# Three pairs of PSUM banks in turn for a windowed attention, and one bank each for its projections and its values

## The chip, the cores and the metric

The kernel runs on one core of one Trainium2 chip. The metric is the device time of one execution in microseconds, here the median of three runs of the kernel before: 1449.96 us (1449.54 to 1451.34).

## What is computed

A trunk of two layers over 1024 latent tokens (a grid of 16 rows and 64 columns) and 256 context tokens, width 1024, 16 heads of 64, all in float32. The change lies in the first layer, a windowed attention with grouped keys, a sink logit for each head and a gate. Cut to what matters:

```python
q, k, v, g = _split_a(u @ w_in)                    # latents; uc likewise, without rotation
q = apply_axial_rope(q, rope); k = apply_axial_rope(k, rope)
for each block of 128 queries and each head:
    s = [q @ k(own block and its two neighbours), masked; q @ k(context); sink]
    p = softmax(s * HEAD_DIM ** -0.5)
    o = p_lat @ v + p_ctx @ v_ctx
y = (o * silu(g)) @ w_out
h = layer_norm(ALPHA * h + gate * y)
```

Context queries look at the context alone. The second layer is a neighbourhood attention of the same build.

## The kernel before, in words

Numbers keep their precision by being split into a high and a low part: a projection makes three matmuls for each 128 rows of its weights (high by high, high by low, low by high, lines 208 to 210).

**Phases of the first layer.** First the modulated tokens `uA`, the keys and part of the values are made; then the attention runs over 8 pairs of heads `p`, each with 10 blocks of 128 tokens (8 of latents, 2 of context) and 2 heads, that is 20 units a pair and 160 in all. Beside the attention of pair `p` run, as filling, the projections of its gate and of the next pair's queries (`gprojA(p)`, `qprojA(p + 1)`). A projection goes over three chunks of tokens (`CHUNKS`: 512, 512 and the 256 of the context), 24 matmuls each, into a PSUM tile `pj`. The chunks of one run are named `pj<j>_<c>`: `pj32` is a query projection, `pj34` the gate projection after it.

**A unit of the attention.** `qkA` makes the scores `S_A` on TensorE (lines 704, 705). `sm_first` scales, masks and reduces them on VectorE (line 317, a custom instruction with the read of its accumulator into `m_A`), then ScalarE takes the exponential (line 324); `sm_second` takes the reciprocal `rs_A` on VectorE (line 328) and GpSimd multiplies (line 329). `sm_transpose` transposes the probabilities on TensorE into `T_A` (line 336), ScalarE copies the high part out (`pth_A`, line 340) and VectorE subtracts for the low part (`ptl_A`, line 342). `pvA_fn` multiplies with the values into a `pvA` tile (line 733), which two blocks share; two ScalarE copies and two VectorE additions (`otmp`, lines 742, 743) empty it. The scores run three units ahead of the transposes (`AHEAD_A = 3`).

**What empties a projection's tile.** For the queries `rope_evac`: VectorE shuffles `pj` into `rb` (line 469), multiplies `pj` by the cosine into `ra` (line 470), GpSimd multiplies `rb` by the sine (line 471), VectorE adds (line 472), and `q_store` makes for each of the two heads a ScalarE cast (line 659) and a VectorE subtraction (line 660) into `qA`. The chunk of the context isn't rotated: `q_store` reads it straight from PSUM. For the gate `g_evac`: ScalarE takes a tanh of `pj` into a tile with the tag `ra` (line 277), VectorE combines it with `pj` into `gA` (line 278). In the first layer the tags `ra` and `rb` have one buffer each.

**PSUM.** [...] The pool `ps` has two tiles of two banks (tag `big`: scores, transposes, sums of the output projection) and four of one bank (tag `one`: projections, values and the rest). A tile gets the buffer that comes free.

**Other work on the same engines.** VectorE and GpSimd work on 48 dot products for the modulation of later steps (`dots`, lines 617, 618, tile `gj`), 7 of them in most pairs.

**What sets the order.** Each engine runs its instructions in the order in which they stand in its program. A scheduler makes that order when the kernel is built, by priorities (order of emission, `merge` mixes attention and filling; `lift(n)` raises what is inside it by n places) and by when it takes buffers to be free. On the chip an instruction waits for semaphores, and all that stands behind it on its engine waits too.

Of the kernel before, what the change touches and what calls it, by code (L numbers as in the profile page):

```python
# [11 lines left out]
F32 = mybir.dt.float32  # L12
# [4 lines left out]
PSUM = bass.MemoryType.PSUM  # L17
DRAM = bass.MemoryType.DRAM

P = 128  # L20
D = 1024
S = 1024
# [8 lines left out]
CHUNKS = ((0, 512), (512, 512), (1024, 256))  # L31
# [2 lines left out]

AHEAD_A, LIFT_A = 3, 80
AHEAD_B, LIFT_B = 3, 40
BARE_B = 108

GATED_LAST = 1 << 20
# [43 lines left out]
def build(tc, i, out):  # L83
    nc = tc.nc
# [7 lines left out]
        return p, st  # L92

    dr = es.enter_context(tc.tile_pool(name="dr", bufs=1, space=DRAM))
    ps = es.enter_context(tc.tile_pool(name="ps", bufs=1, space=PSUM))

    def psbig(name):
        return ps.tile([P, 1024], F32, tag="big", bufs=2, name=name)

    def psone(name):  # L100
        return ps.tile([P, 512], F32, tag="one", bufs=4, name=name)
# [26 lines left out]
    def lift(n):  # L128

        return tc.high_priority(n) if n else nullcontext()  # L130
# [138 lines left out]

        return evac  # L270

    def g_evac(pl, g):


        def evac(pt, t0, n):
            th = pl.tile([P, 512], F32, tag="ra", bufs=1, name="th")
            nc.scalar.activation(th[:, :n], pt[:, :n], AF.Tanh, scale=0.5)
# [181 lines left out]
    adc = pp.tile([P, KT, 2, 2], F32, name="adc")  # L459


    def rope_evac(store, pl, bufs):
        def evac(pt, t0, n):
            if t0 >= S:
                store(pt[:, :n], t0, n)
                return
            a = pl.tile([P, 512], F32, tag="ra", bufs=bufs, name="ra")
            b = pl.tile([P, 512], F32, tag="rb", bufs=bufs, name="rb")
            nc.vector.stream_shuffle(b, pt, SWAP)
            nc.vector.tensor_tensor(a, pt, cos[:, t0 : t0 + n], ALU.mult)  # L470
            nc.gpsimd.tensor_tensor(b, b, sin[:, t0 : t0 + n], ALU.mult)
            nc.vector.tensor_tensor(a, a, b, ALU.add)
            store(a, t0, n)

        return evac
# [125 lines left out]
    def dot_half(h, j):  # L601
        def run():
# [14 lines left out]
            nc.vector.tensor_tensor_reduce(o, t, gh[0], 0.5, 0.0, ALU.mult, ALU.add, accum_out=acc[:, j, 0:1])  # L617
            nc.gpsimd.tensor_tensor(t, t, gh[1], ALU.mult)
            sums.append((t, acc[:, j, 1:2]))
# [24 lines left out]
    pp_st.close()  # L644
    pq, pq_st = pool("attA", "right")


    qA, gA, kA, vA = {}, {}, {}, {}

# [12 lines left out]
        return store  # L662

    def qprojA(p):
        return proj_pieces(pos["Aq", p], uA, CHUNKS, rope_evac(q_store(p), ap_, 1))

    def gprojA(p):
        def gev(pt, t0, n):
            if t0 == 0:
                gA[p] = pq.tile([P, T], F32, tag="gA", bufs=2, name=f"gA{p}")  # L670
            g_evac(ap_, gA[p])(pt, t0, n)

        return proj_pieces(pos["Ag", p], uA, CHUNKS, gev)

# [135 lines left out]
    for p in range(8):  # L810
# [13 lines left out]
        else:  # L824
# [66 lines left out]
    for b in range(10):  # L891
# [315 lines left out]
    for b in range(8):  # L1207
# [31 lines left out]
        for sl in parts:  # L1239
            nc.vector.scalar_tensor_tensor(z[:, sl], z[:, sl], rs[:, 1:2], vecs[3][:, sl], ALU.mult, ALU.add)  # L1240
            dma(grid_rows(out, b)[:, :, sl], z[:, sl])
    ob_st.close()
    ub_st.close()
    wp_st.close()
# [94 lines left out]
```

## Time and profile before

| what | value |
|---|---|
| median of 3 runs | 1449.96 us |
| the profiled execution's own time | 1450.25 us |
| its span, first to last instruction | 1448.5 us |
| granted TensorE clock, mean | 0.994 |
| TensorE busy with matmuls, whole span | 1393.6 us (96%) |
| VectorE busy, whole span | 988.8 us (68%) |
| ScalarE busy, whole span | 733.9 us (51%) |
| GpSimd busy, whole span | 631.7 us (44%) |

In the rows that follow PE is TensorE (PEld its weight loads), DVE VectorE, ACT ScalarE, POOL GpSimd. A group's row gives line, engine, operation, tiles as out<-in, shape and count, then busy us, the mean ns of one, and the engine's idle time just before them with what ended it. A row of the timeline gives start and duration in us. Matmuls are pipelined: a row's duration is longer than the time to the start of the next one.

### The profile page before, as it was taken

Reading aid. Unit: us, or ns where it says so; the run is one execution under the profiler, and the core shown is the slowest. Engines: PE = TensorE matmul, PEld = TensorE weight load, DVE = VectorE, ACT = ScalarE, POOL = GpSimd, SP = SyncE. Lnnn points to the kernel's source line nnn. Section 1 sums busy time; section 2 is a strip of 40 time slices with the busy share of each in tenths; the row PEclk is TensorE's granted clock in tenths of the full one; section 3 lists DMA queues with packets and bytes.
Section 4 is the critical chain, followed back from the end, with each engine's and each line's share of the span. In section 5 each row is a group of like instructions: output and inputs, shape, how many; then the busy total and the mean of one; then the engine's idle time right before and its main releaser. Section 6 shows DMA issues by size and latency. Waiting matters only on the chain. (4 is left out here: it accounts for less than half of the span.)

```text
span 1448.5 us, 25148 instructions
## 1 busy us (share of the span) xinstructions
PE 1393.6 (96%) x8815; PEld 1217.2 (84%) x8816; DVE 988.8 (68%) x2216; ACT 733.9 (51%) x1561; POOL 631.7 (44%) x779
## 2 busy tenths in 40 slices
PE   8998999999999999999999999999999999998995
PEld 5887888888888888788888899888988898887775
DVE  4658887878888789566423766555565565667698
ACT  4336776677676778332222545554454444557310
POOL 0326666666666657233301333333233333336664
PEclk9999999999999999999999999999999999999998
DMA  9472114123222124434278565565555564384353
GB/s 369 172 227 85 60 48 131 45 77 101 68 70 62 56 67 131 133 129 136 75 216 230 156 195 152 150 166 146 168 147 152 146 182 140 102 207 151 114 133 93
DMA packets 117229, 195.05 MB, mean 135 GB/s; under 512 B 9328, under 2 KB 57840, under 8 KB 117104
## 3 DMA queue, kind: packets, MB, share of 16 engines
q1 hardware_dynamic: 117104, 193.45, 44.4%
q8 instruction: 70, 1.15, 0.3%
q14 instruction: 55, 0.45, 0.1%
HBM read 141.51 MB, written 51.90 MB: 134 GB/s over the span
## 5 line engine op out<-in xcount | busy, mean ns | idle before, releaser
L329 POOL TENSOR_SCALAR s_B<-s_B,rs_B 128x640 f32<-128x640 f32 (+1 forms) x128 | 101.1, 790 | 298.0 <-DVE rs_B L328 243.9
L208 PE MATMUL pj<-uBh,wh 128*128 128x512 f32 (+1 forms) x448 | 176.0, 393 | 0.0
L209 PE MATMUL pj<-uBl,wh 128*128 128x512 f32 (+1 forms) x448 | 170.3, 380 | 0.0
L210 PE MATMUL pj<-uBh,wl 128*128 128x512 f32 (+1 forms) x448 | 170.1, 380 | 0.0
L324 ACT ACTIVATE s_B<-s_B,m_B 128x640 f32<-128x640 f32 (+1 forms) x128 | 102.9, 804 | 131.2 <-DVE m_B L317 131.1
L324 ACT ACTIVATE s_A<-s_A,m_A 128x641 f32<-128x641 f32 (+2 forms) x160 | 119.5, 747 | 88.7 <-DVE m_A L317 73.7
L164 POOL TENSOR_TENSOR wl<-wr,wh 128x512 fp32r<-128x512 f32 x64 | 87.7, 1370 | 162.1 <-ACT wh L162 139.8
L329 POOL TENSOR_SCALAR s_A<-s_A,rs_A 128x640 f32<-128x640 f32 (+2 forms) x160 | 126.8, 793 | 58.0 <-DVE rs_A L328 55.7
L317 DVE CUSTOM_DVE_ANT_0 s_A<-S_A,msk,nsk 128x640 f32<-128x640 f32 (+2 forms) x160 | 123.6, 774 | 34.1 <-PE S_A L705 17.7
L342 DVE TENSOR_TENSOR pt_B<-T_B,pt_B 128x640 fp32r<-128x640 f32 (+1 forms) x128 | 100.9, 788 | 61.0 <-ACT pt_B L340 60.6
L208 PE MATMUL pj<-uAh,wh 128*128 128x512 f32 (+1 forms) x384 | 140.0, 365 | 0.0
L209 PE MATMUL pj<-uAl,wh 128*128 128x512 f32 (+1 forms) x384 | 137.8, 359 | 0.0
L210 PE MATMUL pj<-uAh,wl 128*128 128x512 f32 (+1 forms) x384 | 137.5, 358 | 0.0
L342 DVE TENSOR_TENSOR ptl_A<-T_A,pth_A 128x640 fp32r<-128x640 f32 (+2 forms) x160 | 114.0, 713 | 15.3 <-PE pvA L733 7.1
L336 PE MATMUL T_A<-ident,s_A 128*128 128x128 f32 x672 | 101.1, 275 | 12.2 <-DVE m_A L317 8.9
L336 PEld LDWEIGHTS T_A<-ident,s_A 128*128 128x128 f32 x672 | 77.2, 140 | 40.2 <-issue 16.7
L340 ACT CAST pt_B<-T_B 128x640 fp32r<-128x640 f32 (+1 forms) x128 | 84.3, 658 | 47.6 <-PE T_B L336 46.6
L317 DVE CUSTOM_DVE_ANT_0 s_B<-S_B,bias 128x640 f32<-128x640 f32 (+1 forms) x128 | 100.4, 784 | 10.5 <-PE S_B L1036 9.7
L340 ACT CAST pth_A<-T_A 128x640 fp32r<-128x640 f32 (+2 forms) x160 | 96.4, 603 | 16.8 <-PE T_A L336 14.1
L210 PEld LDWEIGHTS pj<-uBh,wl 128*128 128x128 f32 x448 | 84.3, 188 | 16.6
L336 PE MATMUL T_B<-ident,s_B 128*128 128x128 f32 x608 | 88.7, 275 | 9.9 <-DVE pt_B L342 5.0
L242 PE MATMUL pv<-wh,uBh 128*128 128x256 f32 x320 | 92.8, 291 | 3.1 <-ACT wh L162 3.1
(219 smaller groups left out, 3883.6 us busy)
## 6 DMA issues: line engine op xcount, KB each, us to landing
kB<-kdB SPq DMA_DIRECT2D x64, 320.0 KB, 5.2
gw<-in_wadaT SPq DMA_DIRECT2D x48, 256.0 KB, 2.8
vdB<-st SPq DMA_DIRECT2D x20, 512.0 KB, 3.2
vB<-vdB SPq DMA_DIRECT2D x16, 640.0 KB, 4.7
wada<-in_wadaC SPq DMA_DIRECT2D x16, 512.0 KB, 9.6
kdB<-st SPq DMA_DIRECT2D x16, 512.0 KB, 3.0
qdB<-st SPq DMA_DIRECT2D x16, 512.0 KB, 3.5
qB<-qdB SPq DMA_DIRECT2D x32, 256.0 KB, 4.7
```

Of the source, the lines that this page charges most:

```text
L164: e.tensor_tensor(lo, r, f32(hi), ALU.subtract)
L208: mm(pt[:, :n], hi[:, sl], rh, start=kt == 0, stop=False)
L209: mm(pt[:, :n], hi[:, sl], rl, start=False, stop=False)
L210: mm(pt[:, :n], lo[:, sl], rh, start=False, stop=kt == KT - 1)
L242: mm(pt, lh, hi[:, sl], start=kt == 0, stop=False)
L317: nc.vector.tensor_tensor_reduce(outp, sc, in1, scale, init if init is not None else 3e38, ALU.add, ALU.min, accum_out=s.m)
L324: nc.scalar.activation(s.t[:, :n], s.t[:, :n], AF.Exp, bias=s.m, scale=-1.0, accum_out=s.sum)
L329: nc.gpsimd.tensor_scalar(s.t[:, : s.w], s.t[:, : s.w], s.rs, 1.0, ALU.mult, ALU.mult)
L336: nc.tensor.transpose(tp[:, k * P : (k + 1) * P], s.t[:, src * P : (src + 1) * P], ident)
L340: nc.scalar.copy(pt.hi[:, :n, hl, :], tv)
L342: nc.vector.tensor_tensor(pt.lo[:, :n, hl, :], tv, f32(pt.hi[:, :n, hl, :]), ALU.subtract)
```

## The change

PSUM is now cut by a class `Banks` whose layout changes twice. Up to the first layer's attention it is as before: two pairs, four single banks. From the first query projection on it has three pairs and two single banks: score and transpose tiles take the pairs in turn (`big0`, `big1`, `big2`, by order of emission), all projections share one bank (`pj`), and all value products share one (`pv`). When the output projection begins, its first sums take the third pair and the other two go on in turn; after the first block of the output projection the layout is two pairs, taken in turn, and four single banks.

The single `pj` bank is emptied by one ScalarE copy, lifted by 40 places: for queries into the tile `ra` (also for the context's chunk, which had used no `ra` before), for the gate into its slice of `gA`. What used to read PSUM then reads that copy. The tile of the dot products moves from the tag `ra` to `rb`.

```diff
+LIFT_PJ = 40
...
+        def big(self, name):
+            t = self.pairs[self.n % len(self.pairs)]
+            self.n += 1
+            return self.ps.tile([P, 1024], F32, tag=f"big{t}", bufs=1, name=name)
...
+        def one(self, name):
+            if self.ones == 4:
+                return self.ps.tile([P, 512], F32, tag="one", bufs=4, name=name)
+            return self.ps.tile([P, 512], F32, tag=name[:2], bufs=1, name=name)
...
-    def g_evac(pl, g):
+    def g_evac(pl, g, free=False):
...
+            if free:
+                pt, src = g[:, t0 : t0 + n], pt
+                with lift(LIFT_PJ):
+                    nc.scalar.copy(pt, src[:, :n])
...
-    def rope_evac(store, pl, bufs):
+    def rope_evac(store, pl, bufs, free=False):
         def evac(pt, t0, n):
+            if t0 < S or free:
+                a = pl.tile([P, 512], F32, tag="ra", bufs=bufs, name="ra")
+            if free:
+
+                with lift(LIFT_PJ):
+                    nc.scalar.copy(a[:, :n], pt[:, :n])
+                pt = a
             if t0 >= S:
                 store(pt[:, :n], t0, n)
                 return
-            a = pl.tile([P, 512], F32, tag="ra", bufs=bufs, name="ra")
...
-            o = ap_.tile([P, 512], F32, tag="ra", bufs=1, name="gj")
+            o = ap_.tile([P, 512], F32, tag="rb", bufs=1, name="gj")
...
+    banks.st.close()
+    banks.open("psA", 3, 2)
...
-                yA0.extend(psone(f"yA0_{nh}") for nh in range(2))
+                banks.pairs = [0, 1]
+                y = banks.ps.tile([P, 1024], F32, tag="big2", bufs=1, name="yA0")
+                yA0.extend(y[:, sl] for sl in HALVES)
...
+        if b == 0:
+            banks.st.close()
+            banks.open("psB", 2, 4)
```

**Place one: TensorE where the query projection `pj32` of a pair ends and the gate projection `pj34` begins.** `T_A` are transposes, `S_A` scores, `pvA5_6` the value products of blocks 6 and 7 of pair 5. Before:

```order
L208 MATMUL pj32_2_5862<-uAh2_107,wh33_5131 128x256
L209 MATMUL pj32_2_5862<-uAl2_110,wh33_5131 128x256
L210 MATMUL pj32_2_5862<-uAh2_107,wl33_5132 128x256
L208 MATMUL pj34_0_5955<-uAh0_105,wh34_5527 128x512
L209 MATMUL pj34_0_5955<-uAl0_108,wh34_5527 128x512
L210 MATMUL pj34_0_5955<-uAh0_105,wl34_5528 128x512
L336 MATMUL T_A117_5961<-ident_63,s_A117_5831 128x128 x2
L704 MATMUL S_A120_5966<-kA3_0_5384,qA12_5684 128x256
```

The same place in the changed kernel:

```order
L225 MATMUL pj32_2_5910<-uAl2_110,wh33_5174 128x256
L226 MATMUL pj32_2_5910<-uAh2_107,wl33_5175 128x256
L356 MATMUL T_A117_6011<-ident_63,s_A117_5878 128x128 x2
L356 MATMUL T_A118_6048<-ident_63,s_A118_5929 128x128 x2
L224 MATMUL pj34_0_6005<-uAh0_105,wh34_5573 128x512
L762 MATMUL pvA5_6_5939<-pth_A112_5794,vA2_3822 128x256 x5
L762 MATMUL pvA5_6_5939<-ptl_A112_5795,vA2_3822 128x256 x5
L225 MATMUL pj34_0_6005<-uAl0_108,wh34_5573 128x512
L226 MATMUL pj34_0_6005<-uAh0_105,wl34_5574 128x512
```

Four transposes now stand between the two projections, and the ten value products, which stood inside `pj32_2` before, follow the first matmul of `pj34_0`.

**Place two: VectorE, from the rows after the query projection's second chunk `pj32_1` to the last subtraction that reads its `ra`.** `rb` and `ra` are the two tiles of the rotation, `gj` a dot product. Before:

```order
L328 RECIPROCAL rs_A117_5834<-sum_A117_5833 128x1
L470 TENSOR_TENSOR ra_5841<-pj32_1_5707,cos_139 128x512
L317 ISA s_A118_5881,m_A118_5882<-S_A118_5878,msk_141,nsk_142 128x256
L317 ISA m_A118_5882 128x1
L342 TENSOR_TENSOR ptl_A114_5820<-T_A115_5868,pth_A114_5819 128x4x128
L472 TENSOR_TENSOR ra_5841<-ra_5841,rb_5842 128x512
L328 RECIPROCAL rs_A118_5884<-sum_A118_5883 128x1
L743 TENSOR_TENSOR otmp_5856<-pvA5_4_5736,otmp_5856 64x256
L660 TENSOR_TENSOR qA12_5684<-ra_5841,qA12_5684 64x512
L317 ISA s_A119_5918,m_A119_5919<-S_A119_5915,msk_141,nsk_142 128x256
L317 ISA m_A119_5919 128x1
L660 TENSOR_TENSOR qA13_5685<-ra_5841,qA13_5685 64x512
```

The same in the changed kernel:

```order
L362 TENSOR_TENSOR ptl_A114_5867<-T_A115_5916,pth_A114_5866 128x4x128
L496 TENSOR_TENSOR ra_5888<-ra_5888,cos_139 128x512
L337 ISA s_A119_5966,m_A119_5967<-S_A119_5963,msk_141,nsk_142 128x256
L337 ISA m_A119_5967 128x1
L348 RECIPROCAL rs_A118_5932<-sum_A118_5931 128x1
L498 TENSOR_TENSOR ra_5888<-ra_5888,rb_5890 128x512
L772 TENSOR_TENSOR otmp_5904<-pvA5_4_5783,otmp_5904 64x256
L348 RECIPROCAL rs_A119_5969<-sum_A119_5968 128x1
L643 ISA gj_6041,dhalf_733<-gw_6039,gh_3846 128x512
L643 ISA dhalf_733 128x1
L689 TENSOR_TENSOR qA12_5731<-ra_5888,qA12_5731 64x512
L689 TENSOR_TENSOR qA13_5732<-ra_5888,qA13_5732 64x512
```

The last subtraction has moved behind one more reciprocal and a dot product. Ahead of these rows the changed program has, counted from the reduction of `S_A116`: that reduction, a dot product, the reduction of `S_A117`, a `ptl_A`, two reciprocals, the shuffle (now from `ra`) and the reduction of `S_A118`; before, the shuffle stood ahead of the `ptl_A` and of the reciprocal of unit 117.

**Place three: ScalarE at the start of the attention.** `pv-1` are the last value tiles of the phase before, `st` their staging tile for a DMA, `pj8` the first query projection. Before:

```order
L265 ACTIVATE st_902<-pv-1_3_853 128x4x64 x2
L265 ACTIVATE st_965<-pv-1_4_908 128x4x64 x2
L659 CAST qA0_1030<-ra_1024 64x512
L659 CAST qA1_1031<-ra_1024 64x512
L162 CAST wh12_1103<-wr12_995 128x512
L162 CAST wh13_1107<-wr13_997 128x512
```

The same in the changed kernel:

```order
L281 ACTIVATE st_902<-pv-1_3_853 128x4x64 x2
L281 ACTIVATE st_965<-pv-1_4_908 128x4x64 x2
L489 COPY ra_1028<-pj8_0_1003 128x512
L688 CAST qA0_1035<-ra_1028 64x512
L688 CAST qA1_1036<-ra_1028 64x512
L489 COPY ra_1066<-pj8_1_1041 128x512
```

The copies that empty the projections' bank stand behind the staging of the last value tile, and the second behind the casts of the first chunk.

More of the change, by code (lines that the diff above doesn't have):

```diff
@@ L94, in build, with open @@
     dr = es.enter_context(tc.tile_pool(name="dr", bufs=1, space=DRAM))
[L95 to L101, printed above, removed]
+    class Banks:
+        def open(self, name, pairs, ones):
+            self.st = ExitStack()
+            self.ps = self.st.enter_context(tc.tile_pool(name=name, bufs=1, space=PSUM, reuse_waits="tile"))
+            self.pairs, self.ones, self.n = list(range(pairs)), ones, 0
+        def big(self, name):
[6 more added lines that the diff above has]
+            return self.ps.tile([P, 512], F32, tag=name[:2], bufs=1, name=name)
+    banks = Banks()
+    banks.open("ps0", 2, 4)
+    psbig, psone = banks.big, banks.one
     cp = es.enter_context(tc.tile_pool(name="cp", bufs=1, side="left"))
@@ L664, in qprojA @@
     def qprojA(p):
-        return proj_pieces(pos["Aq", p], uA, CHUNKS, rope_evac(q_store(p), ap_, 1))
+        return proj_pieces(pos["Aq", p], uA, CHUNKS, rope_evac(q_store(p), ap_, 1, True))
     def gprojA(p):
@@ L670, in gev @@
                 gA[p] = pq.tile([P, T], F32, tag="gA", bufs=2, name=f"gA{p}")
-            g_evac(ap_, gA[p])(pt, t0, n)
+            g_evac(ap_, gA[p], True)(pt, t0, n)
         return proj_pieces(pos["Ag", p], uA, CHUNKS, gev)
@@ L1241, in build @@
             dma(grid_rows(out, b)[:, :, sl], z[:, sl])
+    banks.st.close()
     ob_st.close()
```

## The prediction

> **What bounds the kernel now.** I read the page first, for the span, and then the view of windows over the first layer's attention, 97 to 592 us.
>
> ```profile
> span 1448.5 us, 25148 instructions
> ```
>
> The profiled execution took 1450.25 us, 1.75 more than its span and 0.3 more than the median of the three runs, 1449.96. A difference made against the span therefore holds for the median as it stands.
>
> ```profile
> core 0: us, PE busy (x) PEld busy (x) DVE busy (x) ACT busy (x) POOL busy (x), PEclk, DMA share, GB/s
> 97.00:592.00 495.00, 474.97 (x3074) 415.45 (x3073) 404.14 (x974) 347.35 (x783) 320.01 (x458) 1.00 0.26 81
> ```
>
> PE is busy for 475 of 495 us, so it sets the pace. DVE follows with 404 (82%) and ACT with 347 (70%), neither with much room. What PE waits for says the view of the groups on PE in that window:
>
> ```profile
> L336 PE MATMUL T_A<-ident,s_A 128*128 128x128 f32 x672 | 101.1, 275 | 12.2 <-DVE m_A L317 8.9 <-POOL gw L618 1.3 <-DVE rs_A L328 0.4
> L705 PE MATMUL S_A<-kA,qA 128*128 128x256 f32 x320 | 84.1, 285 | 1.8 <-DVE ptl_A L342 1.8
> L704 PE MATMUL S_A<-kA,qA 128*128 128x384 f32 (+1 forms) x256 | 84.0, 352 | 5.1 <-DVE ptl_A L342 5.1
> ```
>
> Transposes wait for the reduction `m_A` that reads a score tile, scores for the `ptl_A` that reads a transposed tile. Neither is where the waiting matmul's data come from: these are waits for a pair of banks. They make 8.9 + 1.8 + 5.1 = 15.8 us; all idle time of the three groups is 19.1. That is the most that more pairs can give back, 1.3% of the kernel. No projection stands in the list: with four single banks it never waited for one.
>
> **Three pairs.** In the order of before a transpose tile mostly takes the pair of the scores issued just ahead of it; in the changed order it takes that of scores one unit older. A score tile takes, before as after, the pair of the transposes four units back, so its room hardly grows. I take 16 us as gained, between 10 (the scores' waits stay, and some of the others) and 19.
>
> **One bank for the projections, at the end of each pair.** This is the term that decides. The context's chunk of the query projection is now copied into `ra`, which has one buffer and still holds the chunk before it. So ACT's copy of chunk 2 waits until the last subtraction of chunk 1 has read `ra`, and the gate projection's first matmul waits for that copy. Before, the trace shows this place in the timeline (PE and DVE, pair 5, `pj32` and `pj34`):
>
> ```profile
> 454.89 0.39 PE L210 MATMUL pj<-uAh,wl 128*128 128x512 f32 x1
> ...
> 455.12 0.76 PE L733 MATMUL pvA<-ptl_A,vA 128*128 128x256 f32 x5
> ...
> 455.42 0.74 DVE L469 STREAM_SHUFFLE rb<-pj 128x512 f32<-128x512 f32 x1
> ...
> 455.72 0.28 PE L208 MATMUL pj<-uAh,wh 128*128 128x256 f32 x1
> ...
> 460.79 0.28 PE L210 MATMUL pj<-uAh,wl 128*128 128x256 f32 x1
> ...
> 460.90 0.40 PE L208 MATMUL pj<-uAh,wh 128*128 128x512 f32 x1
> ...
> 461.80 0.69 DVE L660 TENSOR_TENSOR qA<-ra,qA 64x512 fp32r<-64x512 f32 x1
> ```
>
> Chunk 1's last matmul starts at 454.89, the gate projection 6.0 us later, and the last subtraction ends at 462.49, 7.6 us after that matmul. PE had run ahead of it by 1.6 us; now it can't. Costs on DVE and ACT come from the groups of each in the same window:
>
> ```profile
> L617 DVE CUSTOM_DVE_ANT_0 gj<-gw,gh 128x512 f32<-128x512 f32 x48 | 38.1, 794 | 1.4 <-DMA gw<-in_wadaT 1.0
> L743 DVE TENSOR_TENSOR otmp<-pvA,otmp 64x256 f32<-64x256 f32 x80 | 32.9, 412 | 5.8 <-ACT otmp L742 4.5
> L328 DVE RECIPROCAL rs_A<-sum_A 128x1 f32<-128x1 f32 x160 | 25.4, 159 | 23.6 <-ACT s_A L324 22.7
> L660 DVE TENSOR_TENSOR qA<-ra,qA 64x512 fp32r<-64x512 f32 x30 | 24.9, 831 | 4.7 <-ACT qA L659 4.2
> ...
> L342 DVE TENSOR_TENSOR ptl_A<-T_A,pth_A 128x512 fp32r<-128x512 f32 x32 | 21.9, 683 | 0.6 <-ACT th L277 0.3 <-PE pvA L733 0.2
> L317 DVE CUSTOM_DVE_ANT_0 s_A<-S_A,msk,nsk 128x256 f32<-128x256 f32 x32 | 15.4, 480 | 2.0 <-POOL gw L618 0.6 <-PE S_A L705 0.4 <-POOL s_A L322 0.2
> ...
> L317 DVE DVE_READ_ACCUMULATOR2_ANT m_A<- 128x1 f32 x160 | 13.2, 82 | 0.0
> L472 DVE TENSOR_TENSOR ra<-ra,rb 128x512 f32<-128x512 f32 x15 | 11.4, 759 | 0.9 <-POOL rb L471 0.7
> ...
> L469 DVE STREAM_SHUFFLE rb<-pj 128x512 f32<-128x512 f32 x14 | 10.4, 744 | 0.0
> L470 DVE TENSOR_TENSOR ra<-pj,cos 128x512 f32<-128x512 f32 x14 | 9.4, 670 | 0.0
> ```
>
> ```profile
> L277 ACT ACTIVATE th<-pj 128x512 f32<-128x512 f32 x16 | 9.6, 598 | 2.3 <-PE pj L210 2.1
> L659 ACT CAST qA<-pj 64x256 fp32r<-64x256 f32 x15 | 5.4, 361 | 3.9 <-DVE qA L660 3.9
> ```
>
> The changed order puts on DVE, from the reduction of `S_A116` (its matmuls stand just ahead of the last of `pj32_1`) to that last subtraction: four reductions of 0.48 + 0.08, two `ptl_A` of 0.68, four reciprocals of 0.16, two dot products of 0.79 + 0.08, the shuffle 0.74, the multiplication 0.67, the addition 0.76, one `otmp` 0.41, two subtractions of 0.83: 2.24 + 1.36 + 0.64 + 1.74 + 0.74 + 0.67 + 0.76 + 0.41 + 1.66 = 10.2 us without a gap. From 0.3 us after chunk 1's last matmul that ends at 10.5; the copy (0.36, as the cast of 64x256 from PSUM) and two hand-overs bring it to 11.0. PE has less to do meanwhile than before: its 6.0 us less ten `pvA` (455.12 to 455.72 for five, so 1.2), which wait for their own single bank, plus six matmuls of scores and transposes that moved in (0.12 each, as the `pvA`): 5.5. So PE stands for 5.5 us where it stood for 0.2 or so. In three of the seven pairs the order has one dot product less in that row, and in the first and the last PE has one or two us more of other work ahead of the gate projection. I take 4.2 us a pair, 29 in all. The lower bound is the old DVE order: 7.6 + 0.36 + 0.1 against 6.0, 2.1 a pair or 15; the upper is 5.5 a pair or 39. Behind the waiting copy on ACT stand the casts of the context's chunk and of the next `T_A`, and on PE all that follows.
>
> **The other restarts.** Of 47 successions of chunks, 7 are those above and 3 lie at the start; 37 are left. A chunk's last matmul takes 0.39, the copy 0.60 (as the tanh of 128x512 from PSUM), two hand-overs some 0.1: 1.1 us from the start of that matmul. In the changed order PE has mostly six matmuls ahead of the next chunk, two `pvA` and four transposes, 0.7 at the 0.12 of a `pvA`, after 0.23 for the last matmul's own turn (86.38 to 86.61 below): 0.9. That leaves 0.2 where ACT is free at once; at 70% busy, with instructions of half a microsecond to one, it often isn't. I take 0.3 each, 11 us, between 5 (0.15) and 25 (the copy starts half a microsecond late throughout). What hides the rest is those six matmuls; without them each restart would cost 0.9, or 33 us. [...]
>
> **DVE's new sources.** Shuffle, multiplication and the gate's product now read SBUF. The nearest rows: 670 ns for the multiplication from PSUM, 759 for the addition from SBUF alone. I count no gain. [...]
>
> **The start.** `pj8` has no attention beside it. ACT's copy of its first chunk stands behind the staging of the last value tile:
>
> ```profile
> 86.38 0.39 PE L210 MATMUL pj<-uAh,wl 128*128 128x512 f32 x1
> ...
> 86.61 0.39 PE L208 MATMUL pj<-uAh,wh 128*128 128x512 f32 x1
> ...
> 90.31 0.38 ACT L265 ACTIVATE st<-pv-1_4_908 128x256 fp32r<-128x256 f32 x1 [0.49 <-DVE st L266]
> ```
>
> The chunk's last matmul starts at 86.38, the staging ends at 90.69, so the bank is free at 91.4 instead of PE going on at 86.61: 4.8 us. The gate projection after `pj8_2` waits for subtractions behind three score reductions, some 3 more. Part of the 8 comes back, as PE then has projection work left for the waits of the first units. I take 5, between 2 and 9.
>
> **With one answer.** The end of the attention keeps two pairs; the second layer has the same banks as before, taken in strict turn, and its PE order differs in a few dozen rows of 3,600: 0, give or take 2. The `gj` in `rb` waits for nothing new of length: 0.
>
> **The sum.** 29 + 11 + 5 − 16 = +29 us: 1450.25 + 29 = 1479.25 for the profiled execution, 1479 for the median. The low ends together (15 + 5 + 2 − 19) give +3; the high ends (39 + 25 + 9 − 10) +63, which need not come together.
>
> **Rivals.** *Faster.* The bank waits go in full (−19), and the row on DVE is done before PE needs the bank: then only 5 for restarts and 2 for the start remain, −12, 1438. It decides at 5.5 us from chunk 1's last matmul to the last subtraction. For it speaks that 15.8 us of PE's idle time have just that cause; against it the 461.80 row: with no copy ahead DVE took 7.6. [...]
>
> *No change.* All low ends: 1453 at most, 1450 with the staging at the start absorbed. It needs DVE's row to be as short as before although two dot products now lie in it.
>
> *ACT late throughout.* The copies add 32 x 0.60 + 16 x 0.36 = 25 us to ACT's 347. If that makes every restart as late as the upper bound, 36 + 25 + 8 − 12 = +57, 1507. For it: ACT works in order, and many copies stand behind a cast or an exponential; against: the casts they stand behind mostly have their data a microsecond earlier.
>
> **Numbers.** Forecast 0.70, ACT late 0.11, no change 0.08, faster 0.11. A measurement of this kernel tells 0.2% from no change, 2.9 us. Slower by more: 0.70 + 0.11 = 0.81; within: 0.08; faster: 0.11. The range reaches from the no-change case, 1449, to 1503, just short of ACT late; faster and the rest of ACT late are left out.
>
> **What would show it.** In the changed profile PE's projection group (line 224) has some 25 to 40 us of idle time ended by ACT's copies, in seven stretches of 3 to 6 us a pair apart; the copy of 128x256 into `ra` waits for DVE's subtraction; the transposes' wait for `m_A` is nearly gone. I am wrong if the gate projection starts within 1 us of the end of the query projection, if the seven stretches are under 2 us, or if the waits of `T_A` remain.

## The result: 1516.8 us, 4.5% slower

The changed kernel takes 1516.76 us (median of 4 runs, 1511.80 to 1517.76), the kernel before beside it 1449.89. The ratio is 1.0452, 95% interval 1.0429 to 1.0476, so 66 us more. The forecast was 1479 with a range to 1503: the direction was right, the size beyond the range. The profiled execution is the median one, with a span 66.5 us longer. All of it lies in the first layer's attention, from the first query projection on: its last value products end at 657.5 us (588.9 before), and from there to the end of the span it is 857.5 us, where it was 859.6.

The changed kernel's span, and from the view of windows the attention's stretch that was shown of before (us, then busy time of PE, PEld, DVE, ACT and POOL, the granted clock, DMA):

```profile
span 1515.0 us, 25188 instructions
```

```profile
97.00:592.00 495.00, 444.05 (x2737) 387.50 (x2736) 377.22 (x864) 320.14 (x726) 298.90 (x404) 0.95 0.23 67
```

PE is still the busiest engine but works 31 us less of the same 495, at a clock of 0.95 instead of 1.00. All engines do less: no other engine has become the bound, they wait for each other.

**What waits now.** The view of the waits on TensorE from 97 to 660 us, the attention of the changed kernel (line waited for, total, times, longest):

```profile
PE pj L224 <- ACT ra L489: 19.6, 9, 4.4
PE T_A L356 <- POOL s_A L349: 17.0, 9, 2.4
PE pvA L762 <- DVE otmp L772: 10.7, 12, 2.2
PE pj L224 <- ACT gA L295: 2.8, 6, 0.9
PE S_A L734 <- DVE ptl_A L362: 1.5, 3, 1.1
PE S_A L733 <- DVE ptl_A L362: 1.2, 1, 1.2
...
PE T_A L356 <- DVE m_A L337: 0.8, 1, 0.8
```

The waits for a pair of banks are mostly gone: `T_A` for `m_A` fell from 8.9 to 0.8, `S_A` for `ptl_A` from 6.9 to 2.7. Three waits stand in their place: the gate projection for the copy into `ra` (19.6), the transposes for GpSimd's normalized scores, which are their data (17.0), and the value products for the emptying of their one bank (10.7).

From 80 us to the last value products, the sum of all rows of this view is 60.9 us, where it was 19.0 before: 41.9 more.

**A pair's end.** TensorE's timeline of the changed kernel at the end of the query projection of pair 4 (start, duration; in brackets the idle time and its releaser):

```profile
374.34 0.28 PE L226 MATMUL pj<-uAh,wl 128*128 128x256 f32 x1
374.45 0.38 PE L356 MATMUL T_A<-ident,s_A 128*128 128x128 f32 x2
377.21 0.69 PE L356 MATMUL T_A<-ident,s_A 128*128 128x128 f32 x2 [2.38 <-POOL s_A L349]
382.00 0.79 PE L224 MATMUL pj<-uAh,wh 128*128 128x512 f32 x1 [4.10 <-ACT ra L489]
...
384.73 0.63 PE L225 MATMUL pj<-uAl,wh 128*128 128x512 f32 x1
```

The query projection ends at 374.6, the gate projection starts at 382.0; between them are four transposes. TensorE stands twice: 2.38 us ahead of the second two transposes, which wait for their data, and 4.10 us ahead of the gate projection. Over all seven pair ends the stands of the first kind sum to 11.8 us (six, of 1.0 to 2.4) and those of the second to 19.0 (seven, of 1.1 to 4.4), 30.8 together. VectorE, GpSimd and ScalarE at the same place, each from its own timeline:

```profile
373.56 1.32 DVE L496 TENSOR_TENSOR ra<-ra,cos 128x512 f32<-128x512 f32 x1
...
375.28 1.27 DVE L498 TENSOR_TENSOR ra<-ra,rb 128x512 f32<-128x512 f32 x1
...
377.38 1.56 DVE L643 CUSTOM_DVE_ANT_0 gj<-gw,gh 128x512 f32<-128x512 f32 x1
...
378.98 2.51 DVE L689 TENSOR_TENSOR qA<-ra,qA 64x512 fp32r<-64x512 f32 x2
```

```profile
373.04 1.29 POOL L497 TENSOR_TENSOR rb<-rb,sin 128x512 f32<-128x512 f32 x1
374.29 1.71 POOL L180 TENSOR_TENSOR wl<-wr,wh 128x512 fp32r<-128x512 f32 x1
...
377.13 1.26 POOL L180 TENSOR_TENSOR wl<-wr,wh 128x512 fp32r<-128x512 f32 x1
...
379.25 1.69 POOL L644 TENSOR_TENSOR gw<-gw,gh 128x512 f32<-128x512 f32 x1
```

```profile
381.58 0.37 ACT L489 COPY ra<-pj 128x256 f32<-128x256 f32 x1 [2.81 <-DVE qA L689]
```

For the gate projection the chain is the forecast one: subtractions end at 381.49, the copy runs from 381.58 to 381.95, the gate projection starts at 382.00. Note the four long DVE rows: each ends 0.55 us after a GpSimd row has ended (374.88 after 374.33, 376.55 after 376.00, 378.94 after 378.39, 381.49 after 380.94).

**The clock behind a stand.** Three of the seven stretches of the attention in which the granted clock (after the five busy times) is a half, and the sum of all seven, from the view of windows of the changed kernel:

```profile
308.60:315.40 6.80, 5.42 (x20) 4.94 (x21) 4.10 (x7) 2.55 (x7) 4.42 (x5) 0.50 0.16 43
376.90:387.10 10.20, 5.79 (x21) 5.00 (x22) 6.37 (x11) 3.64 (x10) 5.09 (x6) 0.50 0.73 181
448.50:455.30 6.80, 5.09 (x19) 4.71 (x20) 4.21 (x8) 2.88 (x8) 4.75 (x5) 0.50 0.19 58
...
sum 57.80, PE 38.18 PEld 32.96 DVE 38.67 ACT 22.68 POOL 30.04; mean PE 5.45 PEld 4.71 DVE 5.52 ACT 3.24 POOL 4.29
```

TensorE worked for 38.2 of these 57.8 us at half the clock. If that work took half as long at the full clock, the stretches cost some 19 us at most beside the standing itself; this is an estimate, from the pitch of projection matmuls of 128x512 in this trace, 0.42 us (384.73 to 385.15) against 0.23 (387.92 to 388.15, behind the stretch). With the 41.9 us of added waits it makes 61 of the 66 us. Before, there was no such stretch in the attention: its clock from 97 to 592 us is 1.00.

### The profile page after: what moved, and what is told of

The parts are those of the page before. It is cut to its first block, busy times and chain, and to the rows that moved or that the text cites. A ratio compares the mean times of both kernels' runs of the same rounds, so it can differ in the third digit from the quotient of the medians.

```text
span 1515.0 us, 25188 instructions
## 1 busy us (share of the span) xinstructions
PE 1422.1 (94%) x8816; PEld 1236.8 (82%) x8816; DVE 1010.6 (67%) x2216; ACT 757.9 (50%) x1609; POOL 648.0 (43%) x779
## 5 line engine op out<-in xcount | busy, mean ns | idle before, releaser
L349 POOL TENSOR_SCALAR s_A<-s_A,rs_A 128x640 f32<-128x640 f32 (+2 forms) x160 | 131.1, 820 | 119.8 <-DVE rs_A L348 114.5
L224 PE MATMUL pj<-uAh,wh 128*128 128x512 f32 (+1 forms) x384 | 150.6, 392 | 27.1 <-ACT ra L489 24.1
L362 DVE TENSOR_TENSOR ptl_A<-T_A,pth_A 128x640 fp32r<-128x640 f32 (+2 forms) x160 | 112.7, 711 | 23.6 <-ACT pth_A L360 12.3
L356 PE MATMUL T_A<-ident,s_A 128*128 128x128 f32 x672 | 107.0, 277 | 20.1 <-POOL s_A L349 17.0
L356 PEld LDWEIGHTS T_A<-ident,s_A 128*128 128x128 f32 x672 | 81.4, 142 | 35.7 <-POOL s_A L349 22.2
L224 PEld LDWEIGHTS pj<-uAh,wh 128*128 128x128 f32 x384 | 74.6, 194 | 39.4 <-ACT ra L489 28.2
```

The source lines that it names most:

```text
L224: mm(pt[:, :n], hi[:, sl], rh, start=kt == 0, stop=False)
L349: nc.gpsimd.tensor_scalar(s.t[:, : s.w], s.t[:, : s.w], s.rs, 1.0, ALU.mult, ALU.mult)
L356: nc.tensor.transpose(tp[:, k * P : (k + 1) * P], s.t[:, src * P : (src + 1) * P], ident)
L362: nc.vector.tensor_tensor(pt.lo[:, :n, hl, :], tv, f32(pt.hi[:, :n, hl, :]), ALU.subtract)
```

## The experiments

All ratios stand to the kernel before on the same chip; "over" is (ratio − 1) × 1450 us. The changed kernel is 66 over.

| run | ratio, 95% interval | over, us |
|---|---|---|
| e1_ctx_elsewhere | 1.0313 (1.0298 to 1.0328) | 45 |
| h6_changed_gj_ra | 1.0324 (1.0309 to 1.0340) | 47 |
| i1_ctx_and_gj | 1.0294 (1.0271 to 1.0317) | 43 |
| e2_start_only | 1.0411 (1.0391 to 1.0431) | 60 |
| e3_both | 1.0318 (1.0292 to 1.0343) | 46 |
| e5_copies_alone | 1.0175 (1.0158 to 1.0192) | 25 |
| e6_turn_alone | 1.0175 (1.0159 to 1.0191) | 25 |
| e7_copies_dynamic | 1.0139 (1.0118 to 1.0160) | 20 |
| f1_gj_rb | 1.0053 (1.0036 to 1.0070) | 8 |
| f2_turn_gj_ra | 1.0066 (1.0045 to 1.0087) | 10 |
| f3_copies_gj_ra | 0.9996 (0.9984 to 1.0008) | −1 |
| f4_both_gj_ra | 1.0266 (1.0238 to 1.0294) | 39 |
| h1_three_free | 1.0265 (1.0247 to 1.0282) | 38 |
| i2_three_free_shared | 1.0208 (1.0187 to 1.0230) | 30 |
| h3_one_proj_bank | 1.0125 (1.0108 to 1.0142) | 18 |
| h4_one_value_bank | 1.0245 (1.0230 to 1.0260) | 36 |
| c1_two_pairs | 1.0439 (1.0420 to 1.0458) | 64 |
| c2_two_pairs_busy | 1.0470 (1.0446 to 1.0495) | 68 |

The first theory was the prediction's: the copy into `ra` stops TensorE at each pair's end, and the half clock behind it makes up the rest. Its rival: the single banks cost throughout. After the first four runs it stood as half a theory, and the others ask what the rest is.

**Where the time lies.** The profiled executions can be cut at matmuls of the projections: "start", which holds the first pair too, goes from the first matmul of the first query projection to the first of the second pair's gate projection, "six pairs" from there to the first of the eighth pair's gate projection, "last pair" to the end of the last value products. Before, these take 75.1, 365.0 and 67.7 us, and the rest of the span behind them 859.6. The table has what each run takes more, in us, from one execution each:

| run | start | six pairs | last pair | rest |
|---|---|---|---|---|
| changed | 18 | 48 | 2 | −2 |
| i1_ctx_and_gj | 13 | 24 | 6 | −4 |
| f3_copies_gj_ra | −1 | −1 | 2 | −4 |
| h3_one_proj_bank | 10 | 5 | 3 | −1 |
| h4_one_value_bank | 5 | 17 | 5 | 6 |
| f4_both_gj_ra | 11 | 24 | 6 | −3 |
| h1_three_free | 9 | 23 | 4 | −4 |
| i2_three_free_shared | 6 | 24 | −2 | −2 |

The price of a layout that is in use from pair to pair is the column "six pairs".

### The stop at the pair's end: e1, h6, i1

e1 gives the context chunk's copy another landing place, the slice of the next gate tile; h6 takes the line on `gj` back to `ra` (its diff is that of f1 below, backwards); i1 does both.

```diff
-        return proj_pieces(pos["Aq", p], uA, CHUNKS, rope_evac(q_store(p), ap_, 1, True))
+        return proj_pieces(pos["Aq", p], uA, CHUNKS, rope_evac(q_store(p), ap_, 1, lambda: g_tile(p)[:, S:T]))
```

> The changed kernel, but the context chunk's copy of a query projection goes into the context slice of the next pair's gate tile, not into the one buffer of `ra`, so it no longer waits for the last subtraction of chunk 1. Theory (the copy behind the subtraction empties TensorE's work at seven pair ends, and the granted clock then falls to 0.5 for 7 to 10 us): the idle time of the projections' matmuls ended by the copies of the rope falls from 24.1 us to under 8 (what is left is the start), the transposes' wait for GpSimd's normalized scores falls from 17.0 us to under 10, the drops of the clock at 236.9, 308.6, 376.9, 448.5 and 516.8 us go, and the time is 1468 to 1482 us. Rival (single banks that restart slowly everywhere, with ScalarE late throughout): the wait moves to the other copies, and the time stays above 1500 us.

> The changed kernel with one line undone: the dot products' tile keeps the tag `ra`. If that tag costs in the changed kernel what it costs with the strict turn alone: 1499 to 1506 us. If `ra`, now also the landing place of the copies, is held longer by it: 1517 to 1530 us.

> The changed kernel with two parts undone: the context chunk's copy goes into the gate tile's slice, and the dot products' tile keeps `ra`. If the two are two prices: 1471 to 1477 us (23 and 22 us off). If they are one stop, which either takes away: 1488 to 1494 us, with what is left owed to the single banks.

Measured: 1493.75, 1495.19 and 1490.80 us: by the ratios 20, 19 and 23 us off. The two prices are one: either edit takes most of the stop away, and both together little more. The groups of ScalarE's copies of 128x256 into `ra`, in the changed kernel and, second, in h6:

```profile
L489 ACT COPY ra<-pj 128x256 f32<-128x256 f32 x8 | 3.0, 373 | 10.9 <-DVE qA L689 10.9
```

```profile
L489 ACT COPY ra<-pj 128x256 f32<-128x256 f32 x8 | 3.0, 373 | 2.5 <-DVE qA L689 2.2 <-DVE dhalf L643 0.3
```

With the dot products in `ra` the scheduler no longer puts one right ahead of the last subtractions, and ScalarE's idle time before the copy falls by 8.4 us. No theory holds whole: e1 met neither the 1468 to 1482 of the first nor the 1500 of the rival, and the transposes' wait for GpSimd stayed at 16.0 us where under 10 was expected; h6 lies below both of its ranges; i1 fell in that of one stop. In the six pairs i1 takes 24 us less than the changed kernel. 43 us remain in all when the stop is undone from both sides, 13 of them at the start, and at five pair ends of i1 TensorE still stands for 1.4 to 1.8 us ahead of transposes that wait for GpSimd.

### The start: e2, e3

e2 opens the new layout behind the first query projection, which keeps four banks and no copy; e3 is e1 and e2 together.

```diff
-        return proj_pieces(pos["Aq", p], uA, CHUNKS, rope_evac(q_store(p), ap_, 1, True))
+        return proj_pieces(pos["Aq", p], uA, CHUNKS, rope_evac(q_store(p), ap_, 1, p > 0))
...
     merge([], qprojA(0))
+    banks.st.close()
+    banks.open("psA", 3, 2)
```

> The changed kernel, but the first query projection keeps the layout and the evacuation of the kernel before (four single banks, no copy); the three pairs and the single banks begin behind it. Theory (the start's stop of 4.45 us at 87.2 us comes from the copy of `pj8_0` behind the staging of the last values, and it and the two waits of 2.3 and 2.4 us behind it bring two drops of the clock, 6.8 and 10.2 us long): all these go, the seven pair ends stay as they are, and the time is 1500 to 1506 us, 11 to 17 less than the changed kernel's. Rival (the start's waits come from the unfilled attention, not from the copy): the waits of the first transposes stay, and the time is within 4 us of 1516.8.

> Both edits at once: the context chunk's copy goes into the gate tile's slice, and the first query projection keeps the old layout and evacuation. Theory: the gains add, since the places are apart: 1454 to 1468 us, with no drop of the clock to 0.5 in the first layer's attention longer than 4 us; what is then left over the kernel before is the restart at each chunk of the single banks, less what three pairs take away. Rival (the single banks and ScalarE's copies cost throughout): above 1490 us.

Measured: 1507.56, 6 us off by the ratios and 9 by the medians. That lies outside both ranges of e2, and its interval touches that of the changed kernel; but the projections' wait for the rope's copies fell from 24.1 us to 19.5 over the whole span, about the 4.5 of the start, so that stop is real. e3 took 1494.10, no less than e1 alone. The view of the waits on TensorE in e3 has this row, which the changed kernel and e1 lack:

```profile
PE S_A L735 <- DVE qA L688: 4.3, 1, 4.3
```

With the start undone, the first scores wait there for `qA` instead. The other runs that keep the first query projection in the old way have the row too (e2, f4, h1 and h3 with 4.3 us, h4 and i2 with 1.8), and e2 gained all the same, so why e3 gains nothing isn't settled. The expectation for e3 fell: 46 us stand without either stop.

### Copies, turn and the dot products' tag in the old layout

Six kernels have the kernel before's two pairs and four single banks. e5 has copies, strict turn and `gj` in `rb`; e6 turn and `gj`; e7 copies and `gj`; f2 the turn alone, f3 the copies alone (the context's in the gate tile); f1 is the kernel before with one line changed. First the edit by which e7 and f3 give up the turn, then the line on the tag (e5, e6, e7, f1):

```diff
-            return self.ps.tile([P, 1024], F32, tag=f"big{t}", bufs=1, name=name)
+            return self.ps.tile([P, 1024], F32, tag="big", bufs=2, name=name)
...
-            o = ap_.tile([P, 512], F32, tag="ra", bufs=1, name="gj")
+            o = ap_.tile([P, 512], F32, tag="rb", bufs=1, name="gj")
```

> The layout of PSUM of the kernel before (two pairs, here taken in turn, and four single banks) with the copies of the change added, the context's in the gate tile's slice: it prices the copies and the strict turn without the single banks. Theory (the copies themselves are cheap where a second bank is free): 1447 to 1456 us, no wait of the projections' matmuls for a copy over 1 us in a row. Rival (ScalarE's 48 copies and what they delay cost the time): 1475 us or more, with waits for ScalarE spread over all units.

> The kernel before with only the strict turn: score and transpose tiles take the two pairs by order of emission, no copies, four single banks. The previous kernel of this kind with both copies and turn took 26 us more than before. If the turn is the cause: 1466 to 1476 us, with the transposes waiting for VectorE's `ptl_A` as there. If the copies are: 1448 to 1454 us.

> The kernel before with only the copies (the projections' tile is emptied by one ScalarE copy, the context chunk's into the gate tile's slice); the two pairs are taken as they come free, four single banks. If the copies are what costs: 1466 to 1476 us, with waits of the transposes for VectorE and ScalarE. If the strict turn is: 1448 to 1454 us.

> The kernel before with one line changed: the tile of the dot products takes the tag `rb` instead of `ra`. Strict turn alone and copies alone each took some 20 to 25 us more, and both together no more than that; this line is what both had in common. If it is the cause (VectorE's program is ordered anew around `gj`): 1464 to 1472 us. If it costs nothing, as the prediction said: 1446 to 1452 us.

> Strict turn alone with the dot products left in `ra`. If `gj` in `rb` was the cause of its 25 us: 1448 to 1455 us; if the strict turn was: 1466 to 1474 us.

> Copies alone, pairs taken as they come free, with the dot products left in `ra`. If `gj` in `rb` was the cause of its 20 us: 1447 to 1453 us; if the copies were: 1462 to 1470 us.

Measured: 1473.75, 1472.11, 1466.82, 1455.81, 1458.14 and 1447.22 us. e5 gave 25 us where 1447 to 1456 was expected; e6 and e7, meant to say which part it was, each kept 20 to 25. What both had in common was `gj`. By itself the line costs 8 us, with the copies 21 (e7 against f3), with the turn 16 (e6 against f2). With four single banks the copies cost nothing (−0.2% to +0.1%); the turn of two pairs costs 10 us. f1 and f2 fell between their ranges, f3 met that of free copies. The price of `gj` is no constant: without the stop the line costs 3 us (e1 against i1) to 8 (e3 against f4).

Why does a tile that nothing reads cost time? Its tag decides when the scheduler may place the dot products on VectorE. The group of the subtractions in f1, where before it had 24.9 us and 831 ns:

```profile
L660 DVE TENSOR_TENSOR qA<-ra,qA 64x512 fp32r<-64x512 f32 x30 | 38.5, 1284 | 1.1 <-ACT qA L659 0.2
```

The same instruction on the same operands, in another order, takes 13.6 us more in all. From 455 to 470 us in f1 it falls beside GpSimd's work: two of these subtractions take 2.49 us from 456.01 on, while GpSimd runs a multiplication from 455.95 to 457.24. On TensorE the scores' wait for `ptl_A` rose from 6.9 to 13.1 us.

### Single banks and the third pair: h3, h4, f4, h1, i2

All have the copies (the context's in the gate tile), `gj` in `ra` and the first query projection in the old way. h3 and h4 have two pairs as they come free, with one bank for the projections (h3) or the values (h4) and three for the rest. f4 has three pairs in turn and one bank each, h1 three pairs as they come free, i2 the same with the two single banks lent to both kinds. The core of h4, and behind it that of i2:

```diff
+            if name[:2] == "pv":
+                return self.ps.tile([P, 512], F32, tag="alone", bufs=1, name=name)
+            return self.ps.tile([P, 512], F32, tag="rest", bufs=3, name=name)
...
-            return self.ps.tile([P, 512], F32, tag=name[:2], bufs=1, name=name)
+            return self.ps.tile([P, 512], F32, tag="one", bufs=self.ones, name=name)
```

> Two pairs taken as they come free, one bank for the projections alone, and three for the rest; copies as there, dot products in `ra`. If the single projection bank is the cause: 1470 to 1485 us. If the values' bank is: 1448 to 1456 us.

> Two pairs taken as they come free, one bank for the values alone, and three for the rest; copies as there, dot products in `ra`. If the single bank of the values is the cause (its products stand in one block behind the ends of `otmp`): 1470 to 1485 us. If the projections' bank is: 1448 to 1456 us.

> Three pairs, the context chunk's copy in the gate tile's slice, the first query projection in the old way, and the dot products left in `ra`. If `gj` in `rb` accounts for some 20 of its 46 us: 1468 to 1478 us. If the transposes' waits at the pair ends and the one bank of the values are what is left: 1488 to 1496 us.

> Three pairs taken as they come free, not in turn; all else as the three pairs with the dot products left in `ra`, the context chunk's copy in the gate tile's slice and the first query projection in the old way (1488.6 us). If the strict turn causes the 38 us that are left: 1450 to 1465 us. If the single banks do: 1478 to 1488 us, with the value products waiting for `otmp` as before.

> Three pairs taken as they come free, and the two single banks lent to projections and values alike, not one to each kind; copies, dot products and start as in the run with three free pairs (1486 us). If one bank to each kind is what costs: 1455 to 1470 us. If two banks are too few, however they are lent, or the value products stand in blocks all the same: 1480 to 1490 us.

Measured: 1466.82 (h3), 1483.70 (h4), 1488.57 (f4), 1486.16 (h1) and 1478.51 us (i2). h3 and i2 fell between their ranges, h4, f4 and h1 in those of the single banks. Both single banks cost, the values' most: h4 is 36 us over, of which some 6 lie behind the attention (below) and don't occur in the changed kernel, 5 at the start and 17 in the six pairs. Of h3's 18 us, 10 lie at the start, where the new layout begins and the first scores wait 4.3 us for `qA`; in the six pairs one bank for the projections costs 5. The 17 and the 5 together are near the 24 of f4, which has both single banks. Waits on TensorE in h4, 97 to 612 us:

```profile
PE S_A L735 <- DVE ptl_A L362: 10.1, 8, 1.7
PE T_A L356 <- DVE m_A L337: 7.4, 11, 1.8
PE pvA L764 <- DVE otmp L774: 6.9, 14, 1.1
```

and in its view over the whole span, the one behind the attention:

```profile
PE yA L439 <- DVE z L942: 7.1, 1, 7.1
```

In f3, with four single banks, the same view has no wait of the value products. How the wait spreads shows TensorE's timeline of h4 at a pair's end:

```profile
418.92 0.86 PE L764 MATMUL pvA<-pth_A,vA 128*128 128x256 f32 x5 [1.05 <-DVE otmp L774]
419.61 0.76 PE L764 MATMUL pvA<-ptl_A,vA 128*128 128x256 f32 x5
420.21 0.64 PE L764 MATMUL pvA<-pth_A,vA 128*128 128x256 f32 x4
420.69 0.40 PE L225 MATMUL pj<-uAl,wh 128*128 128x512 f32 x1
422.39 0.39 PE L735 MATMUL S_A<-kA,qA 128*128 128x256 f32 x1 [1.30 <-DVE ptl_A L362]
```

Fourteen value products stand in one block behind the two copies and two additions that empty the bank. The scores behind them wait for a pair, whose `ptl_A` stands on VectorE behind the second of these additions, a dot product and the two subtractions of the context's chunk.

f4 and h1 have the same total, but not the same waits. In h1, and in i2 on the value products, the context's copy stops TensorE at the pair ends again, though it has a landing place of its own. The views of waits of h1 and of i2, 80 to 640 us, and TensorE and ScalarE at one pair end of h1:

```profile
PE pj L226 <- ACT gA L493: 13.6, 6, 3.3
```

```profile
PE pvA L766 <- ACT gA L493: 14.0, 6, 3.6
```

```profile
362.76 0.80 PE L226 MATMUL pj<-uAh,wh 128*128 128x512 f32 x1 [3.24 <-ACT gA L493]
```

```profile
360.69 1.24 ACT L689 CAST qA<-ra 64x512 fp32r<-64x512 f32 x2
361.95 0.37 ACT L775 COPY otmp<-pvA 64x256 f32<-64x256 f32 x1
362.34 0.37 ACT L493 COPY gA<-pj 128x256 f32<-128x256 f32 x1
```

The last matmul of the query projection ends at 359.0; the copy stands on ScalarE behind two casts and a copy and starts at 362.34. In f4 the wait for this copy is 2.8 us in all. So the equal totals don't show that the turn of three pairs is free, and i2 doesn't show that two shared banks are too few: its 8 us less than h1 lie outside the six pairs, and 14.0 us of its waits are for this copy.

### The third pair and the stand: c1, c2

c1 is the changed kernel with two pairs instead of three. c2 adds, at six pair ends, 24 matmuls whose result nothing reads, into the empty pair; it computes more than the reference asks.

```diff
-    banks.open("psA", 3, 2)
+    banks.open("psA", 2, 2)
...
+            t = banks.ps.tile([P, 1024], F32, tag="big2", bufs=1, name="dm")
+            for _ in range(24):
+                mm(t[:, 0:512], hi[:, 0:P], rh, start=True, stop=True)
```

> The changed kernel with two pairs in turn instead of three in the first layer's attention (the third is kept empty until the output projection). It is the base for the next run, and prices the third pair in the presence of the stops. Theory (the stops at the pair ends come from the copy into `ra`, not from the pairs): the gate projection's wait for ScalarE stays, 20 us or more in total, with drops of the clock to 0.5 behind it, and the time is 1510 to 1545 us. Rival (the third pair's strict turn is what costs): under 1500 us.

> The same with two pairs, and at six pair ends 24 matmuls of 128x512 that nothing reads, into the empty pair, ahead of the gate projection: 144 matmuls of 0.227 us, 32.7 us of work added where TensorE stands. Theory (the clock falls because TensorE stands, and costs 3 to 4 us a pair end): the drops to 0.5 at these six ends go, matmuls behind them run at full pitch, and the time is 8 to 20 us below the two pairs without them, although more is computed. Rival (the fall of the clock costs nothing or comes for another reason): the drops stay or the time is the same or up to 10 us more.

Measured: 1510.95 and 1513.44 us. In c1 the projections' wait for the rope's copies stayed, at 15.4 us (4.5 of them at the start) instead of the 20 expected. c1 and the changed kernel have overlapping intervals (1.0420 to 1.0458, 1.0429 to 1.0476): in the changed kernel the third pair gives nothing back that can be measured. c2's expected gain didn't come, the time is as its rival had it; but c2 is a weak test of the clock: in c1 the order at these ends is another, the gate projection waits 1.7 us at most there, and only two of the six ends had a fall of the clock (at 176.4 and 374.3 us, 3.4 us each). In c2 both are gone; the mean granted clock of the profiled execution is 0.985 in c1 and 0.991 in c2. What it shows is the stand: 32.7 us of added matmuls raised the median by 2.5 us (the intervals overlap), while all waits on TensorE, from 80 us to the last value products, fell from 48.1 to 28.9. So most of the added matmuls ran in time that was standing still.

## Why the prediction was right in direction and wrong in size

**Three pairs, −16 expected.** The waits named went, 8.9 to 0.8 and 6.9 to 2.7 us, 12.3 together, but no gain in time came of it: c1, with two pairs, takes no longer, and other waits stand in their place, for data (17.0) and for the values' bank (10.7). How much the third pair is worth where nothing else stands isn't known; no run has both single banks with two pairs and no stop.

**The end of each pair, +29 expected.** The mechanism held, and its size: 30.8 us of stands at the seven ends, and 19 to 23 us less time when it is undone. The split was not foreseen: 11.8 of the 30.8 are transposes that wait for GpSimd, which the prediction counted as work to be done meanwhile. The gate's own stands are not all of 3 to 6 us, as foretold: three were 4.1 to 4.4 us, the other four 1.1 to 1.9 (one is shown in the last section). The DVE row that was to end 10.5 us after chunk 1's last matmul ended 12.3 us after it, which stands in the same timeline of TensorE as

```profile
369.20 0.40 PE L226 MATMUL pj<-uAh,wl 128*128 128x512 f32 x1
```

The four rows shown above took 6.66 us where the rates of before give 3.88 (0.67, 0.76, 0.79 and 1.66).

**The other restarts, +11 expected, 25 at most.** Not too small: behind the start and the pair ends the projections wait 3.4 us for copies in the changed kernel (2.8 for those of the gate), and one bank for the projections alone costs 5 us in six pairs (h3).

**The values' single bank, no term.** This is the step that failed by most. The prediction had ten value products "which wait for their own single bank" in its working of the pair's end, and put the price of that bank at nothing. In the changed kernel the value products wait 10.7 us for it; alone it costs 17 us in six pairs and about 22 with the last (h4).

**DVE's new sources, 0 expected.** Wrong as to VectorE, harmless as to the time by itself. Groups on VectorE in the changed kernel from 97 to 660 us:

```profile
L496 DVE TENSOR_TENSOR ra<-ra,cos 128x512 f32<-128x512 f32 x15 | 15.5, 1032 | 0.0
L298 DVE SCALAR_TENSOR_TENSOR gA<-th,gA 128x512 f32<-128x512 f32 x16 | 13.5, 843 | 2.0 <-ACT th L297 2.0
L689 DVE TENSOR_TENSOR qA<-ra,qA 64x256 fp32r<-64x256 f32 x16 | 10.3, 642 | 2.8 <-ACT qA L688 2.4
L298 DVE SCALAR_TENSOR_TENSOR gA<-th,gA 128x256 f32<-128x256 f32 x8 | 6.6, 822 | 0.2
```

Reading PSUM they took 670, 678, 422 and 418 ns. With both sources in SBUF they take 1032, 843, 642 and 822: (362 × 15 + 165 × 16 + 220 × 16 + 404 × 8) ns = 14.8 us more of VectorE. f3 has the same longer rows (the first at 1021 ns) and the time of before, so longer rows alone cost nothing; they count where TensorE waits for them, as at the pair's end. The multiplications (L496) come in two groups: six of the 15 took 0.67 to 0.69 us, and nine, each begun 0.5 to 0.6 us after GpSimd's multiplication by the sine, took 1.23 to 1.32 and ended 0.55 after it. Before, reading PSUM, all 14 took 0.66 to 0.68, seven of them begun just as long after the same GpSimd instruction. The four long rows above end 0.55 us after a GpSimd row too. The prediction went by two mean lengths. No run takes GpSimd's part by itself.

**The start, +5 expected, 9 at most.** Too small: the start takes 18 us more (table). TensorE stands 4.45 us for the first copy, then 2.33 and 2.45 us for the data of the first transposes, and two of the seven stretches of half clock, 17 us, lie there. Undoing the copy gives 6 to 9 us while the other stops stand (e2) and nothing beside e1 (e3).

**`gj` in `rb`, 0 expected.** Wrong: 8 us by itself, 16 to 21 with turn or copies, 19 in the changed kernel, 3 to 8 where the stop is undone. It waits for nothing; it changes VectorE's order.

**The end and the second layer, 0.** Right, −2 us. **ScalarE late throughout** came nearest in its number, 1507, by luck: the restarts that it makes late wait 3.4 us in the changed kernel, and with four banks (f3) the copies cost nothing. As a mechanism it is real in h1 and i2, where the context's copy stands behind casts.

**The clock** had no term. It fell to 0.50 behind stands at five of the seven pair ends and twice at the start, and made these dearer by the estimated 19 us at most, where the forecast fell 37 short. No run takes it alone, so its share isn't settled.

Together, by the runs: of the 48 us in the six pairs the stop is 24 (i1), and the remaining 24 are what f4 pays for both single banks and h4 and h3 pay for one each (17 and 5). That this rest is the banks' is shown by these sums, not wait for wait: f4 waits at other places than h4 and h3. The start makes 18 us, of which 6 to 9 are the copy's; the cause of the rest there is open.

## What to carry to other kernels

A bank fewer is not priced by how long one copy empties it: ask what the scheduler will put in a block ahead of and behind it, and price each kind of tile that loses a bank, not only the one that the change speaks of. A stand costs more than its length where the clock falls behind it, here by an estimated 19 us at most beside 41.9 of added waits. A copy that frees one resource early must not land in a buffer with one owner. And a tag is a constraint on the order: a tile that nothing reads can move work on another engine, so it is tried by itself.

## What the hardware showed that was not expected

The granted clock fell to a half after stands much shorter than the 4.10 us of the pair's end above; there too it fell at 376.9, before that stand began, 2.07 us into the one of 2.38. TensorE's timeline of the changed kernel at 308 us, where the clock is a half from 308.6, and of the kernel before in the second layer, where it is a half from 1332.6:

```profile
307.67 0.44 PE L356 MATMUL T_A<-ident,s_A 128*128 128x128 f32 x2 [1.84 <-POOL s_A L349]
309.98 0.79 PE L224 MATMUL pj<-uAh,wh 128*128 128x512 f32 x1 [1.87 <-ACT ra L489]
```

```profile
1332.72 1.30 PE L336 MATMUL T_B<-ident,s_B 128*128 128x128 f32 x5 [2.11 <-POOL gB L1077]
```

```profile
1332.60:1336.00 3.40, 3.28 (x13) 2.92 (x13) 1.23 (x3) 2.67 (x7) 2.79 (x4) 0.50 0.49 193
```

In the first case the clock fell after 1.84 us and the first half microsecond of the next stand, in the second after 1.99 us of one stand of 2.11. In the changed kernel the stretches are 6.8 and 10.2 us long in the attention and 3.4 behind it (656.7 to 660.1), and the one of before shown above is 3.4. Of the 3.4 us ahead of these three falls TensorE had stood for 2.07, 2.33 and 1.99. At the first and the last pair end of the changed kernel, where the stands were 1.0 to 1.4 us, no fall came: the clock is 1.00 from 155 to 186 us and from 578 to 595. How long a stand may be without a fall isn't shown beyond these cases.
